# Sums of output weights: made in the prompt attention, or as a GpSimd task in the first half of the projection

## The chip, the cores and the metric

The kernel runs on one core of one Trainium2 chip. The metric is device time in microseconds (us) from the first to the last instruction of the program, with what lies around it; smaller is better. Three runs of the kernel before took 2386.06, 2387.06 and 2393.02 us, median 2387.06.

Engines are called by their names in the profile: PE is TensorE (matmuls, PEld its weight loads), DVE VectorE, ACT ScalarE, POOL GpSimd, SP SyncE, which here only issues DMA transfers.

## What is computed

One layer of a decoder with four head groups, for a prompt of 2048 tokens and for 8 samples of 4 tokens with 8192 cached tokens each. The reference, cut to what matters here:

```python
h = rms_norm(x, pre_g)
z = h @ w_in                                   # (2048 + 32) x 1024 @ 1024 x 5632
ca, cb, cg, pu, pg, q, k, v, sg, mq, mg = split(z)
y_c, conv_new = conv_branch(ca, cb, ...)       # causal depthwise convolution
y_p, pool_new = pool_branch(pu, ...)           # pooling windows 2, 4, 8, 16
y_s = sb_fn(q, k, v, sb_bias)                  # stick-breaking attention, 8 heads x 64
y_m = mem_attend(mq, mk, mv)                   # 4 heads x 128 into 256 memory tokens
mix = concat([y_c * silu(cg), y_p * silu(pg), y_s * silu(sg), y_m * silu(mg)])
out = rms_norm(mix @ w_out, post_g)            # 2048 x 1024 output weights
return x + out
```

The samples attend to cached keys and values, which are gathered page by page through a page table. The last product, `mix @ w_out`, is made with seven products of half-size blocks in place of eight (Strassen's scheme in Winograd's form), so that some products need sums and differences of blocks of `w_out`. These are the sums of output weights that the change moves.

## The kernel before

**Stages.** The program runs through four stages, one behind the other on TensorE.

1. The projection (`z_groups`, called from `main`), up to about 1480 us. It goes over two halves of the prompt tokens, called parts 0 and 1, and in each over groups of 128 output columns: q, k and v first, then per chunk c of 0 to 3 the kinds ca, cb, pu, cg, pg, mg, and mq with sg. For each group `load_w` loads the weights (`wr`, on SyncE's queue), `split_w` splits them into a high and a low part (`whi` on ACT, `wlo` on POOL or, for some, DVE), and `mm3` makes three products per block of 128 rows (L242). Beside it run small generators, the tasks. `Tasks.step` advances each of them once per half group; among them are `mem_attend`, the pooling branch, the convolution and `later_stats`.
2. The attention of the samples (`sample_stages`) is woven into the projection. One of its 64 steps n takes about 18 us: two gathers of cached keys (`kt`, L924), their transposes on DVE (`T`, L957), score matmuls (`sSA`, L970), weights, four gathers of cached values (`vt`, L924) and the values matmuls (`sO`, L1009). The gathers are indirect DMAs that POOL issues in its own order. There is one set of four `vt` buffers, so that the gathers for step n are issued after the values matmuls of step n - 1.
3. The prompt attention (`sb_prompt`), from about 1490 to 1975 us: four head pairs, each with four blocks of 512 query rows. A block's score matmuls are L1253, the gates `gam` and `be` on ACT L1257 and L1258, the scans `E` on DVE L1323 and L1326, the products `be` on POOL L1335, the transposes AT on PE L1346, their evictions `at` L1350 and L1352, the values matmuls `av` L1362. `sbo` (L1367) ends a block.
4. The output product, to the end.

**Side work.** Beside the prompt attention a generator `side_work` is advanced by a fixed amount of attention cost (`PACE`). It holds, in this order: the end of the sample attention, `weight_sums`, the output weights of the first product (`out_weights(1, ...)`: a load `wor`, a cast `wohi` on ACT at L1611 and a difference `wolo` on POOL at L1616, eight times), the first mixed rows, and the convolution's normalisation.

**`weight_sums`.** For each of eight j it loads two blocks of 128 rows of `w_out` (`ws`, two tiles of 4 KB per partition, L1569), makes four sums of 128 x 512 elements on POOL (L1575), and stores the two tiles into a DRAM tensor `wsd` (L1578). `wsd` is read from about 1976 us on, in the output product.

**What sets the order.** TensorE's instructions run in the order in which the program is written. On the other engines and on the DMA queues a scheduler sets the order when the program is built; at run time each engine takes its instructions strictly in that order, and so does each DMA queue. An instruction that waits holds all behind it on its engine.

**Shared buffers.** `k4` hands out tiles of 4 KB per partition from a set of four (`K4 = 4`). `later_stats`, the q and k evictions, and `mem_attend` (`mh`, `pT`, `pL`) use them. `state["att"]` counts the calls of `mem_attend` that have not ended.

Of the kernel before, what the change touches and what calls it, by code (L numbers as in the profile page):

```python
# [8 lines left out]
F32 = mybir.dt.float32  # L9
# [4 lines left out]
ALU = mybir.AluOpType  # L14
# [4 lines left out]
P = 128  # L19
# [68 lines left out]
def kernel(  # L88
# [161 lines left out]
    tasks = Tasks()  # L250
# [7 lines left out]
    def k4(name, shape, dt):  # L258
        return st.tile(shape, dt, tag="k4", name=name, bufs=K4)
# [179 lines left out]
    def half_rows(j):  # L439

        k = 4 + j if j < 4 else j - 4
        return slice(P * (8 + j), P * (9 + j)), slice(P * k, P * k + P)

    def params_and_histories(mp):
        prow = mp.tile([P, 512], F32, tag="ht", name="prow")
# [340 lines left out]
    def z_groups(part, groups, between=None):  # L786

        for g in groups:
            last = part == 0 and g is GROUPS[0][-1]
            fill_w()  # L790
            if last:
                X["free"] = 0
                tasks.add(x_stream(1, XA, lambda n: k4(n, [P, D], F32)))
            opened = [z_open(part, kind, c) for kind, c in g]
            cols = COLS[part]
            for ti, (c0, c1) in enumerate(cols):
                for j, (kind, c) in enumerate(g):
                    while X["done", part] < c1:
                        yield 0.0
                    ps = z_tile(f"z{part}{kind}{c}_{ti}")  # L800
                    half = 2.56 * (c1 - c0) / 512
                    for _ in mm3(ps, *wsplit[(part, kind, c)], xhi, xlo, c0, c1):
                        yield half
                    z_evac(part, kind, c, ti, c0, c1, ps, opened[j])
                    if ti == len(cols) - 1:
                        z_close(part, kind, c, opened[j])
                        del wsplit[(part, kind, c)]
                        fill_w()
                    if last and j == 1:
# [749 lines left out]
    FACTORS = {1: 11, 2: 21, 3: 22}  # L1559
    SUMS = {4: (0, 0), 7: (0, 1), 6: (1, 0), 5: (1, 1)}  # L1560

    def weight_sums(wsp):

        ts = {}
        for j in range(9):
            if j < 8:
                ts[j] = [wsp.tile([P, 2, 512], F32, tag="ws", name=f"ws{j}_{n}", bufs=6) for n in range(2)]
                for t, r in zip(ts[j], half_rows(j)[::-1]):
                    sp.dma_start(t.rearrange("p b n -> p (b n)"), w_out0[r])  # L1569
            yield  # L1570
            if j:
                t, u = ts.pop(j - 1)
                for o, a, b, op_ in ((t[:, 1], t[:, 1], u[:, 1], ALU.subtract), (u[:, 1], u[:, 1], u[:, 0], ALU.subtract),
                                     (u[:, 0], t[:, 1], u[:, 0], ALU.add), (t[:, 0], t[:, 0], u[:, 0], ALU.subtract)):
                    pool.tensor_tensor(out=o, in0=a, in1=b, op=op_)  # L1575
                    yield
                for n, o in enumerate((t, u)):
                    sp.dma_start(wsd[n, j - 1], o)  # L1578
                yield

    def weight_load(prod, j, raw):

        if (prod, j) in seconds:
# [333 lines left out]
    def side_work():  # L1917
        nonlocal opm, conv
        with tc.tile_pool(name="sm", bufs=1, side="left", reuse_waits="tile") as sm2:
            yield from sample_end(sm2, side_ps, S)  # L1920
        with tc.tile_pool(name="wsp", bufs=1, side="left", reuse_waits="tile") as wsp:
            yield from weight_sums(wsp)
        opm = ox.enter_context(tc.tile_pool(name="opm", bufs=1, side="left", reuse_waits="tile"))
        yield from out_weights(1, opm, pool)
        while (3, 0) not in flags:
            yield
        for x in lead_:
            out_load(x)
# [12 lines left out]
        while "centered" not in flags:  # L1941
            next(conv)
            yield
# [195 lines left out]
```

## Time and profile before

| what | value |
|---|---|
| profiled execution | 2387.03 us |
| its span, first to last instruction | 2385.3 us |
| mean granted clock of TensorE | 0.987 |
| TensorE busy | 2283.3 us, 96% |
| VectorE busy | 1717.9 us, 72% |
| GpSimd busy | 1282.7 us, 54% |
| ScalarE busy | 1120.3 us, 47% |
| DMA, mean over the span | 234 GB/s |
| sums of output weights on GpSimd | 32, first at 1563.0, last at 1672.2 us |

How to read it: times inside a run count from the first instruction of the span. The profiled execution has 1.7 us around its span. Busy times of engines overlap. Rows of a timeline give start, duration, engine, line, operation, what is written from what, and in square brackets how long the engine sat idle before it and what ended that. Rows of a table of stretches give, for each engine, the busy time and in parentheses the instructions, then the granted clock of TensorE, the busy share of the DMA engines and their rate.

### The profile page before, as it was taken

What the parts mean: (1) busy time and instruction counts of PE and PEld (TensorE: products, weight loads), DVE (VectorE), ACT (ScalarE), POOL (GpSimd) and SP (SyncE); (2) the same over time, 40 slices, a digit from 0 to 9 for tenths busy, and PEclk for the clock granted to TensorE, in tenths of its full rate; (3) what the DMA queues carried; (4) which work ended last, traced back from release to release, by engine and by line L of the source; (5) the groups of instructions that cost most, each with busy time, mean ns of one, the idle gap of its engine ahead of it and who ended that gap; (6) DMA issues with size and microseconds to landing.
All of it is one profiled execution on the core that took longest, in us unless ns stands there. A gap on an engine that the chain in (4) does not pass through costs nothing. (4 is left out here: it accounts for less than half of the span.)

```text
span 2385.3 us, 42238 instructions
## 1 busy us (share of the span) xinstructions
PE 2283.3 (96%) x16024; PEld 1774.9 (74%) x16024; DVE 1717.9 (72%) x2428; ACT 1120.3 (47%) x1947; POOL 1282.7 (54%) x1322
## 2 busy tenths in 40 slices
PE   7999999999999999999999999799999999989996
PEld 7898888888888677777777777455555557878875
DVE  5342796969657564577787868878888966777897
ACT  5322243242442222234242424788899875444554
POOL 3454545555565555545546462699877763531231
PEclk9999999999999999999999999899999999999999
DMA  6678977878778899987877875667443206866774
GB/s 212 196 257 290 349 270 259 286 249 291 246 262 316 296 327 331 327 283 260 305 263 262 269 268 150 165 201 215 123 107 79 78 19 218 289 196 207 238 236 162
DMA packets 336869, 557.94 MB, mean 234 GB/s; under 512 B 27986, under 2 KB 212434, under 8 KB 320267
## 3 DMA queue, kind: packets, MB, share of 16 engines
q1 hardware_dynamic: 281290, 286.53, 38.7%
q0 software_dynamic: 55376, 268.72, 31.8%
q8 instruction: 126, 2.06, 0.3%
q14 instruction: 77, 0.62, 0.1%
HBM read 465.09 MB, written 90.68 MB: 233 GB/s over the span
## 5 line engine op out<-in xcount | busy, mean ns | idle before, releaser
L957 DVE STREAM_TRANSPOSE T<-kt 128x1024 f32<-128x1024 f32 x256 | 308.7, 1226 | 190.0 <-PE sSA L970 179.0
L924 POOL DMA_INDIRECT vt<-in_cache_v_dram,idv x256 | 252.8, 987 | 261.6 <-PE sO L1009 200.6
L610 DVE SCALAR_TENSOR_TENSOR cacc<-U,par,cacc 128x512 f32<-128x512 f32 x480 | 359.9, 750 | 11.0
L1335 POOL TENSOR_TENSOR be<-be,E 128x512 f32<-128x512 f32 (+3 forms) x316 | 300.7, 963 | 70.0 <-DVE E L1326 22.5
L1326 DVE TENSOR_TENSOR_SCAN E<-gam,cr,ZM 128x513 f32<-128x513 f32 x192 | 233.3, 1264 | 23.3 <-ACT gam L1257 13.9
L924 POOL DMA_INDIRECT kt<-in_cache_k_dram,idk x128 | 128.5, 1004 | 195.0 <-DVE T L957 152.1
L1346 PEld LDWEIGHTS AT<-ident,be 128*128 128x128 f32 x1082 | 118.1, 143 | 137.0 <-ACT at L1352 40.9
L1959 PE MATMUL acc<-wohi,mh 128*128 128x512 f32 (+1 forms) x480 | 193.3, 403 | 1.5 <-ACT mh L1704 0.8
L1257 ACT ACTIVATE gam<-S,nbias_bc 128x1024 f32<-128x1024 f32 (+1 forms) x158 | 170.2, 1077 | 47.3 <-ACT be L1258 15.4
L1959 PE MATMUL acc<-wolo,mh 128*128 128x512 f32 (+1 forms) x480 | 189.0, 394 | 0.0
L1346 PE MATMUL AT<-ident,be 128*128 128x128 f32 x1082 | 161.4, 286 | 20.9 <-DVE at L1350 9.1
L1253 PE MATMUL S<-kT,Q 128*128 128x512 f32 (+1 forms) x632 | 176.5, 403 | 4.8 <-ACT be L1258 4.8
L1959 PE MATMUL acc<-wohi,ml 128*128 128x512 f32 x448 | 176.9, 395 | 4.1 <-DVE ml L1715 4.1
L1258 ACT ACTIVATE be<-S,bias_bc 128x1024 f32<-128x1024 f32 (+1 forms) x158 | 169.1, 1070 | 0.0
L1362 PE MATMUL av<-at,V 128*64 128x512 f32 (+3 forms) x640 | 153.1, 558 | 3.9 <-DVE sbo L1367 3.9
L970 PE MATMUL sSA<-T,W 128*32 128x128 f32 x4096 | 140.5, 277 | 2.3 <-DVE T L957 1.4
L970 PEld LDWEIGHTS sSA<-T,W 128*32 128x32 f32 x4096 | 105.6, 110 | 37.4 <-issue 30.8
L1009 PE MATMUL sO<-vt,saT 128*32 128x512 f32 x1024 | 122.3, 592 | 0.0
L1253 PEld LDWEIGHTS S<-kT,Q 128*128 128x128 f32 x632 | 106.7, 196 | 18.2 <-ACT be L1258 5.4
L1323 DVE TENSOR_TENSOR_SCAN E<-gam,ZM 128x384 f32<-128x384 f32 (+1 forms) x124 | 94.6, 811 | 33.1 <-ACT gam L1257 25.7
L1352 ACT COPY at<-AT 128x512 f32<-128x512 f32 x192 | 108.9, 650 | 20.1 <-PE AT L1346 19.9
L1715 DVE TENSOR_TENSOR ml<-mr,mh 128x512 fp32r<-128x512 f32 x108 | 87.2, 812 | 30.7 <-ACT mh L1704 30.6
(577 smaller groups left out, 6039.9 us busy)
## 6 DMA issues: line engine op xcount, KB each, us to landing
Q<-qd SPq DMA_DIRECT2D x64, 256.0 KB
mr<-mixd SPq DMA_DIRECT2D x32, 512.0 KB
mr<-mixd SPq DMA_DIRECT2D x48, 256.0 KB
xtp<-in_x_prompt_dram SPq DMA_DIRECT2D x16, 512.0 KB
kT<-kd SPq DMA_DIRECT2D x64, 128.0 KB
ws<-in_w_out_dram SPq DMA_DIRECT2D x16, 512.0 KB
wsd<-ws SPq DMA_DIRECT2D x16, 512.0 KB
msd<-mr SPq DMA_DIRECT2D x32, 256.0 KB
```

Of the source, the lines that this page charges most:

```text
L610: dve.scalar_tensor_tensor(out=ps, in0=U[:, a + k : a + k + H], scalar=wd[:, k : k + 1], in1=ps, op0=ALU.mult, op1=ALU.add)
L924: pool.indirect_dma_start(out=dst, out_offset=None, in_=rows, in_offset=bass.IndirectOffsetOnAxis(ap=idx, axis=0))
L957: S["turn"] = dve.transpose(T[:, 2 * hh : 2 * hh + 2].rearrange("p s j t -> p (s j t)"), kt[:, 2 * hh : 2 * hh + 2].rearrange("p s j d -> ...
L970: pe.matmul(sSs[n][32 * g : 32 * g + 32, P * ml : P * (ml + 1)], lhsT=W[:, jj, :], rhs=T[:, :, jj, :], start=i == 0, stop=i == 3, tile_pos ...
L1253: pe.matmul(S[:, j, :w], lhsT=Q[:, x, P * (q2 + j) : P * (q2 + j + 1)], rhs=kt[:, :w], start=x == 0, stop=x == 1)
L1257: act.activation(out=ga, in_=S[:, :, :w], func=AF.Sigmoid, bias=nbias_bc[:, h : h + 1], scale=-1.0)
L1258: act.activation(out=be, in_=S[:, :, :w], func=AF.Sigmoid, bias=bias_bc[:, h : h + 1])
L1326: dve.tensor_tensor_scan(out=E[:, j][:, ::-1], data0=g_[:, j][:, ::-1], data1=ZM[:, 0:1].to_broadcast([P, 513]), initial=carry[hh, q2][:, ...
L1335: pool.tensor_tensor(out=be[:, j, :m], in0=be[:, j, :m], in1=E[:, j, 513 - w : 513 - w + m], op=ALU.mult)
L1346: pe.transpose(ap_[:, P * qt : P * (qt + 1)], A[hp, qb, kc, hh, qt][:, P * r : P * (r + 1)], ident)
L1362: pe.matmul(av[64 * hh : 64 * hh + 64, c], lhsT=V[:, 4 * kc + r, 64 * hh : 64 * hh + 64], rhs=ats.pop((hp, qb, kc, r, hh))[:, c], start=dg ...
L1959: pe.matmul(o[:rows], lhsT=m[a][:, k, :rows], rhs=W[prod, 4 * h + k][w], start=not cont and h == k == n == 0, stop=h == 1 and k == 3 and n ...
```

## The change

`weight_sums` becomes a task of the projection. It takes its tiles from the four shared 4 KB buffers in place of a pool of its own, starts a pair only when no `mem_attend` is open, waits three steps after the loads, and makes the same four sums and two stores per pair. `main` adds the task after the group mg of chunk 0 in part 0; `side_work` no longer calls it, and goes from the end of the sample attention straight to `out_weights(1, ...)`.

```diff
+    def weight_sums():
+
+        for j in range(8):
+            while state["att"]:
+                yield
+            t, u = [k4(f"ws{j}_{n}", [P, 2, 512], F32) for n in range(2)]
+            for o, r in zip((t, u), half_rows(j)[::-1]):
+                sp.dma_start(o.rearrange("p b n -> p (b n)"), w_out0[r])
+            for _ in range(3):
+                yield
+            for o, a, b, op in ((t[:, 1], t[:, 1], u[:, 1], ALU.subtract), (u[:, 1], u[:, 1], u[:, 0], ALU.subtract),
+                                (u[:, 0], t[:, 1], u[:, 0], ALU.add), (t[:, 0], t[:, 0], u[:, 0], ALU.subtract)):
+                pool.tensor_tensor(out=o, in0=a, in1=b, op=op)
+                yield
+            for n, o in enumerate((t, u)):
+                sp.dma_start(wsd[n, j], o)
...
-    def weight_sums(wsp):
-
-        ts = {}
-        for j in range(9):
-            if j < 8:
-                ts[j] = [wsp.tile([P, 2, 512], F32, tag="ws", name=f"ws{j}_{n}", bufs=6) for n in range(2)]
-                for t, r in zip(ts[j], half_rows(j)[::-1]):
-                    sp.dma_start(t.rearrange("p b n -> p (b n)"), w_out0[r])
-            yield
-            if j:
-                t, u = ts.pop(j - 1)
...
     def main():
         yield from z_groups(0, GROUPS[0][4:12])
         tasks.add(later_stats())
-        yield from z_groups(0, GROUPS[0][12:])
+        yield from z_groups(0, GROUPS[0][12:17])
+        tasks.add(weight_sums())
+        yield from z_groups(0, GROUPS[0][17:])
...
             yield from sample_end(sm2, side_ps, S)
-        with tc.tile_pool(name="wsp", bufs=1, side="left", reuse_waits="tile") as wsp:
-            yield from weight_sums(wsp)
         opm = ox.enter_context(tc.tile_pool(name="opm", bufs=1, side="left", reuse_waits="tile"))
```

The new function adds 17 lines near the start, so that lines behind it have numbers higher by 17 in the changed kernel, and behind the place of the old one numbers lower by 2.

TensorE's instructions stand in the same order before and after. The first place is GpSimd's queue in the projection, chunk 1 of part 0, around the values gathers of step 11 of the sample attention (`vt11`), before:

```order
L924 DMA kt12_0_4006<-in_cache_k_dram,idk_1378 128x2048
L924 DMA kt12_1_4093<-in_cache_k_dram,idk_1378 128x2048
L233 TENSOR_TENSOR wlo0pu1_4122<-wr0pu1_3865,whi0pu1_4123 128x1024
L727 TENSOR_TENSOR U0_1_3950<-U0_1_3950,sg0cb1_0_4157 128x384
L924 DMA vt11_0_4184<-in_cache_v_dram,idv_1379 128x1024
```

and after:

```order
L456 TENSOR_TENSOR ws1_0_4118<-ws1_0_4118,ws1_1_4119 128x512
L941 DMA kt12_1_4103<-in_cache_k_dram,idk_1378 128x2048
L233 TENSOR_TENSOR wlo0pu1_4136<-wr0pu1_3875,whi0pu1_4137 128x1024
L456 TENSOR_TENSOR ws2_0_4308<-ws2_0_4308,ws2_1_4309 128x512
L456 TENSOR_TENSOR ws2_1_4309<-ws2_1_4309 128x512
L456 TENSOR_TENSOR ws2_1_4309<-ws2_0_4308,ws2_1_4309 128x512
L456 TENSOR_TENSOR ws2_0_4308<-ws2_0_4308,ws2_1_4309 128x512
L744 TENSOR_TENSOR U0_1_3960<-U0_1_3960,sg0cb1_0_4171 128x384
L941 DMA vt11_0_4199<-in_cache_v_dram,idv_1379 128x1024
```

The four sums of ws1 (the last of them is shown) have come ahead of the gather kt12_1, those of ws2 ahead of vt11. In the same way eight sums, of ws3 and ws4, now stand ahead of the next set vt12, four of ws5 ahead of vt13, one of ws0 ahead of vt7, and eight of ws6 and ws7 around kt19_1, ahead of vt18.

The second place is SyncE's queue at the same time; `mixd` stores rows of the memory attention, `mvn` and `wr` are loads of the projection. Before:

```order
L532 DMA mixd_63<-mo0_0_384_4028 128x3x128
L671 DMA mvn0_1_4947<-mvd_68 128x512
L532 DMA mixd_63<-mo0_0_768_4071 128x2x128
L226 DMA wr0pg1_4126<-in_w_in_dram 128x8x128
L226 DMA wr0mg1_4286<-in_w_in_dram 128x8x128
```

and after:

```order
L549 DMA mixd_63<-mo0_0_384_4038 128x3x128
L451 DMA ws1_0_4118<-in_w_out_dram 128x1024
L451 DMA ws1_1_4119<-in_w_out_dram 128x1024
L451 DMA ws2_0_4308<-in_w_out_dram 128x1024
L549 DMA mixd_63<-mo0_0_768_4081 128x2x128
L451 DMA ws2_1_4309<-in_w_out_dram 128x1024
L459 DMA wsd_70<-ws1_0_4118 128x1024
L459 DMA wsd_70<-ws1_1_4119 128x1024
L688 DMA mvn0_1_5002<-mvd_68 128x512
L451 DMA ws3_0_4494<-in_w_out_dram 128x1024
L226 DMA wr0pg1_4140<-in_w_in_dram 128x8x128
```

Loads of ws1 to ws3 and stores of ws1 have come between the store of the memory attention and the weight load wr0pg1, which now stands behind two stores that wait for GpSimd.

The third place is GpSimd's queue in the prompt attention, head pair 0, the first products of its fourth block. Before:

```order
L1575 TENSOR_TENSOR ws0_0_15534<-ws0_0_15534,ws0_1_15535 128x512
L1335 TENSOR_TENSOR be0_3_3_0_0_15608<-be0_3_3_0_0_15608,E0_3_3_0_0_15670 128x127
L1575 TENSOR_TENSOR ws0_1_15535<-ws0_1_15535 128x512
L1331 COPY cr0_3_3_0_0_15673<-E0_3_3_0_0_15670 128x2
L1335 TENSOR_TENSOR be0_3_3_0_0_15608<-be0_3_3_0_0_15608,E0_3_3_0_0_15670 128x255
L1575 TENSOR_TENSOR ws0_1_15535<-ws0_0_15534,ws0_1_15535 128x512
L1575 TENSOR_TENSOR ws0_0_15534<-ws0_0_15534,ws0_1_15535 128x512
L1575 TENSOR_TENSOR ws1_0_15583<-ws1_0_15583,ws1_1_15584 128x512
L1335 TENSOR_TENSOR be0_3_3_0_2_15637<-be0_3_3_0_2_15637,E0_3_3_0_2_15701 128x383
```

and after:

```order
L1352 TENSOR_TENSOR be0_3_3_0_0_15684<-be0_3_3_0_0_15684,E0_3_3_0_0_15751 128x127
L1348 COPY cr0_3_3_0_0_15754<-E0_3_3_0_0_15751 128x2
L1352 TENSOR_TENSOR be0_3_3_0_0_15684<-be0_3_3_0_0_15684,E0_3_3_0_0_15751 128x255
L1352 TENSOR_TENSOR be0_3_3_0_2_15713<-be0_3_3_0_2_15713,E0_3_3_0_2_15782 128x383
L1348 COPY cr0_3_3_0_2_15785<-E0_3_3_0_2_15782 128x2
L1352 TENSOR_TENSOR be0_3_3_0_2_15713<-be0_3_3_0_2_15713,E0_3_3_0_2_15782 128x511
L1614 TENSOR_TENSOR wolo1_0_15738<-wor1_0_15614,wohi1_0_15737 128x512
L1352 TENSOR_TENSOR be0_3_3_1_0_15748<-be0_3_3_1_0_15748,E0_3_3_1_0_15813 128x127
```

The sums are gone from between the products; a `wolo` of the first output product has come in, the first of eight that stood in head pairs 1 and 2 before.

More of the change, by code (lines that the diff above doesn't have):

```diff
@@ L1560 @@
     SUMS = {4: (0, 0), 7: (0, 1), 6: (1, 0), 5: (1, 1)}
-    def weight_sums(wsp):
-        ts = {}
-        for j in range(9):
-            if j < 8:
-                ts[j] = [wsp.tile([P, 2, 512], F32, tag="ws", name=f"ws{j}_{n}", bufs=6) for n in range(2)]
-                for t, r in zip(ts[j], half_rows(j)[::-1]):
-                    sp.dma_start(t.rearrange("p b n -> p (b n)"), w_out0[r])
-            yield
-            if j:
-                t, u = ts.pop(j - 1)
[L1573 to L1579, printed above, removed]
     def weight_load(prod, j, raw):
```

## The prediction

> **What bounds the kernel now.** I read the page's first part, then a table of stretches, then the waits of TensorE, then the timelines around the two places that the change touches.
>
> ```profile
> PE 2283.3 (96%) x16024; PEld 1774.9 (74%) x16024; DVE 1717.9 (72%) x2428; ACT 1120.3 (47%) x1947; POOL 1282.7 (54%) x1322
> ```
>
> TensorE is busy for 2283.3 of 2385.3 us, and the change gives it no work and takes none away. So the time moves only by what TensorE waits, and GpSimd matters where it makes TensorE wait. The next rows are stretches of the span: two of the projection, three of the prompt attention in which the sums of output weights run now, and two of the same attention without them.
>
> ```profile
> core 0: us, PE busy (x) PEld busy (x) DVE busy (x) ACT busy (x) POOL busy (x), PEclk, DMA share, GB/s
> 400.00:500.00 100.00, 100.00 (x900) 89.25 (x899) 92.30 (x134) 37.33 (x71) 57.72 (x55) 1.00 0.79 268
> 790.00:800.00 10.00, 7.52 (x63) 5.24 (x65) 6.73 (x10) 2.49 (x6) 0.16 (x1) 0.83 0.56 194
> 1563.00:1583.40 20.40, 19.55 (x108) 11.35 (x106) 13.43 (x14) 18.06 (x24) 20.08 (x25) 1.00 0.73 226
> 1583.40:1633.20 49.80, 45.10 (x236) 25.91 (x235) 35.90 (x42) 40.59 (x55) 46.88 (x56) 0.93 0.65 202
> 1666.70:1705.00 38.30, 34.35 (x181) 19.66 (x181) 29.18 (x35) 31.10 (x41) 31.25 (x40) 0.96 0.43 118
> 1781.60:1814.40 32.80, 32.32 (x182) 18.79 (x181) 28.80 (x35) 31.18 (x42) 25.48 (x34) 1.00 0.32 78
> 1814.40:1857.00 42.60, 42.01 (x238) 24.16 (x237) 35.24 (x42) 40.28 (x56) 32.49 (x43) 1.00 0.31 77
> ```
>
> Two things are to be seen. In the projection (400 to 500) TensorE is busy all the time at full clock, so every microsecond that it is made to wait there is added to the time. In the attention equal work takes unequal time: the third block of query rows of a head pair has 181 or 182 matmul records in 1666.7 to 1705.0 and in 1781.6 to 1814.4, the fourth 236 and 238 in 1583.4 to 1633.2 and in 1814.4 to 1857.0. The slow ones are those in which GpSimd is full (46.88 of 49.80) and in which the clock falls below 1.00. The waits of TensorE name GpSimd, first for 1555 to 1680, then for 1680 to 1800:
>
> ```profile
> PE AT L1346 <- POOL be L1335: 6.9, 8, 1.2
> ```
>
> ```profile
> PE AT L1346 <- POOL be L1335: 0.3, 1, 0.3
> ```
>
> The transposes AT wait for the products `be`, and those stand behind the sums in GpSimd's queue.
>
> **The change part by part.** *Removed from the attention.* These are the sums, then the products `wolo` that follow them:
>
> ```profile
> L1575 POOL TENSOR_TENSOR ws<-ws,ws x24: 1270/1286/1302, 1563.0 to 1672.2; 128x512 f32<-128x512 f32 x24
> ...
> L1575 POOL TENSOR_TENSOR ws<-ws x8: 1275/1286/1311, 1564.6 to 1669.4; 128x512 f32<-128x512 f32 x8
> ```
>
> ```profile
> L1616 POOL TENSOR_TENSOR wolo<-wor,wohi x7: 1281/1284/1299, 1706.3 to 1782.9; 128x512 fp32r<-128x512 f32 x7
> ```
>
> 32 sums of 1.286 us are 41.2 us of GpSimd. What they cost TensorE is the difference of equal blocks: 49.8 - 42.6 = 7.2 us, 38.3 - 32.8 = 5.5 us, and for the part of the earlier block after the first sum its idle time, 20.40 - 19.55 = 0.9 us. Together 13.6 us, lost clock included. In the place of the sums comes the next step of the side work, eight casts on ScalarE and eight `wolo` on GpSimd, seven of which stand from 1706 on now, where they cost nothing that the blocks show (1781.6 to 1857.0 hold the last of them). Earlier they come more densely. Bounds: nothing, as there, or the price of a sum, 13.6 / 32 = 0.43 us each, 3.4 us. I take 1.5, between the two. Gain: 13.6 - 1.5 = 12.1 us.
>
> *Added to the projection.* GpSimd's queue also holds the gathers of cache rows there (`kt`, `vt`). A `vt` gather waits until the values matmuls `sO` of the step before have freed its four buffers, and the next `sO` needs it. So what stands ahead of a gather in the queue decides whether TensorE waits. The heaviest place has twenty sums (ws1 to ws5) among these rows of GpSimd:
>
> ```profile
> 381.78 0.94 POOL L924 DMA_INDIRECT kt<-in_cache_k_dram,idk  x1 [3.99 <-DVE T L957]
> 383.54 2.40 POOL L233 TENSOR_TENSOR wlo0pu<-wr0pu,whi0pu 128x1024 fp32r<-128x1024 f32 x1 [0.82 <-ACT whi0pu L232]
> 387.58 0.87 POOL L727 TENSOR_TENSOR U<-U,sg0cb 128x384 f32<-128x384 f32 x1 [1.64 <-ACT sg0cb L725]
> 389.90 0.98 POOL L924 DMA_INDIRECT vt<-in_cache_v_dram,idv  x1 [1.46 <-PE sO L1009]
> ...
> 393.69 0.94 POOL L924 DMA_INDIRECT vt<-in_cache_v_dram,idv  x1 [0.30 <-issue]
> ...
> 399.84 0.98 POOL L924 DMA_INDIRECT kt<-in_cache_k_dram,idk  x1 [3.07 <-DVE T L957]
> ...
> 408.23 1.01 POOL L924 DMA_INDIRECT vt<-in_cache_v_dram,idv  x1 [4.03 <-PE sO L1009]
> ...
> 426.32 0.94 POOL L924 DMA_INDIRECT vt<-in_cache_v_dram,idv  x1 [2.55 <-PE sO L1009]
> ```
>
> The values matmuls that use the gathers of 408.23 and of 426.32, and one that I need later, then the transfer rate microsecond by microsecond from 400 to 440:
>
> ```profile
> 424.16 1.90 PE L1009 MATMUL sO<-vt,saT 128*32 128x512 f32 x16
> ...
> 442.41 1.90 PE L1009 MATMUL sO<-vt,saT 128*32 128x512 f32 x16
> ...
> 542.70 1.90 PE L1009 MATMUL sO<-vt,saT 128*32 128x512 f32 x16
> ```
>
> ```profile
> GB/s 401 221 172 360 270 211 330 118 37 33 242 315 205 295 315 311 340 438 422 229 16 16 16 223 338 81 332 390 304 365 347 336 418 406 410 434 420 390 299 262
> ```
>
> Four gathers start 3.8 us apart from first to last (389.90 to 393.69). The set of 408.23 and the `kt` gather behind it, issued 1.25 us after the last, at about 413.3, have landed when the rate falls to 16 at 420: a flight of 6.8 us. So the slack between landing and use is 424.16 - 412.0 - 6.8 = 5.4 us for the set of 408.23, and 442.41 - 430.1 - 6.8 = 5.5 for that of 426.32. Now the queue's delay against before, with GpSimd's idle time in brackets taken off. Eight sums of 1.29 stand ahead of 389.90; their first loads are issued behind this row of SyncE
>
> ```profile
> 373.73 0.37 SPq L532 DMA_DIRECT2D mixd<-mo  x1
> ```
>
> at about 374.5, and land by the same flight at 381.3, so that the idle 3.99 ahead of 381.78 buys only 0.5. Delay 10.3 - 0.5 - 0.82 - 1.64 - 1.46 = 5.9. Eight more stand ahead of 408.23: 5.9 - 3.07 + 10.3 - 4.03 = 9.1; TensorE is late by 9.1 - 5.4 = 3.7. Four more (5.1) ahead of 426.32: 9.1 - 2.55 + 5.1 = 11.7; TensorE is late by 11.7 - 5.5 = 6.2 in all. This is the larger of the two, not their sum, since a late TensorE gives the queue time to catch up. The next set has no sums ahead of it, and the delay ends there. SyncE's queue holds the weight loads of the projection behind the stores of the sums, thus behind GpSimd. I add nothing for them, since a whole group of matmuls lies between such a load and its use; if that cover is gone, the split of the weights on GpSimd comes late by the same delay, and TensorE by no more than it.
>
> Clock: the row of 790 has one wait, 10.00 - 7.52 = 2.5 us, and a mean clock of 0.83 over 10 us, so a wait of this size can cost another 1.7 us. Of my two waits (3.7, then 2.5 more) both could; what the first costs comes off the second, so at most one 1.7 is left. The Trainium skill, in TensorE: Matmul & The Clock Gate, Part 1, says that the clock halves only after an idle window of some 3.4 us; by that rule the row of 790 would stand at 1.00, and the trace differs. By the rule the term is 0, by the row up to 1.7 us.
>
> Traffic: the page gives the transfers of the sums.
>
> ```profile
> ws<-in_w_out_dram SPq DMA_DIRECT2D x16, 512.0 KB
> wsd<-ws SPq DMA_DIRECT2D x16, 512.0 KB
> ```
>
> They fall beside the gathers now. The price on a gather lies between nothing and the bytes that overlap it at the highest rate of the row above: stores of ws3 and ws4 and loads of ws5 are six of 0.52 MB, 3.1 MB at 438 GB/s, 7.2 us. I take 1.8 for traffic and clock together, near the low end, since the same row has pauses of 16 to 37 to fill. Sum for this place: 6.2 + 1.8 = 8.0 us.
>
> The first pair (ws0) stands ahead of a gather that idles longer:
>
> ```profile
> 305.38 0.94 POOL L924 DMA_INDIRECT vt<-in_cache_v_dram,idv  x1 [5.00 <-PE sO L1009]
> ```
>
> One sum and the wait for its load hold it back by some 5 us (the load is issued some 3 us before this row, and flies 6.8), about the slack of the other sets, 5.4: 0, and as much as the load comes later if it does. The last pairs (ws6, ws7) stand around these:
>
> ```profile
> 524.89 0.87 POOL L727 TENSOR_TENSOR U<-U,sg0cb 128x384 f32<-128x384 f32 x1 [2.81 <-ACT sg0cb L725]
> 527.26 0.98 POOL L924 DMA_INDIRECT vt<-in_cache_v_dram,idv  x1 [1.51 <-PE sO L1009]
> 530.36 0.95 POOL L924 DMA_INDIRECT vt<-in_cache_v_dram,idv  x1 [2.12 <-PE z0cb L242]
> ```
>
> 10.3 - 2.81 - 1.51 - 2.12 = 3.9 us of delay against a slack of 542.70 - 532.9 - 6.8 = 3.0 (two more gathers, 1.25 apart, follow 530.36): TensorE waits 0.9, call it 1.0; with two overlapping stores of each pair, 2.1 MB at 438 GB/s, up to 5.8.
>
> **Sum.** The profiled execution took 2387.03 us (span 2385.3 and 1.7 around it), and the median of the runs is 2387.06, so both are the same base. 2387.0 - 12.1 + 8.0 + 1.0 = 2383.9: 2384 us.
>
> **The rivals.** *The gathers stay hidden (faster).* If a gather alone flies faster than 6.8 us (2.1 MB at 438 GB/s is 4.8), the slack of the last set is 7.5 and TensorE is late by 11.7 - 7.5 = 4.2; with no traffic term, nothing at the last pairs, and `wolo` as cheap as it is now, 2387.0 - 13.6 + 4.2 = 2377.6. For it: the pauses in the rate. Against it: the flight was read with the queue as full as it is.
>
> *The transfers collide (slower).* Loads and stores of the sums share the DMA engines with the gathers where the rate is already near 438. Then the heavy place costs 6.2 + 7.2 + 1.7 = 15.1 and the last pairs 5.8 + 1.7 = 7.5, and 2387.0 - 12.1 + 22.6 = 2397.5. It decides from 19.3 us of loss on (12.1 + 7.2). The Trainium skill, in DMA: Bandwidth & Descriptors, Queues, rings and completion order, says that each engine takes turns between queues, packet by packet. By that rule a gather loses at most as many bytes of time as the other queue has moved meanwhile, which is this rival's price.
>
> *The room in the attention is filled again.* If the dense `wolo` and casts hold `be` as the sums did, the gain is 5 and the time 2387.0 - 5 + 9.0 = 2391. For it: ScalarE is busy 40.28 of 42.60 in the undisturbed block. Against it: that block lost nothing.
>
> **How the numbers follow.** A measurement of this kernel tells 0.3%, 7.2 us, from no change. Forecast (gain and loss nearly cancel) 0.44, hidden gathers 0.28, collision 0.20, filled room 0.08. The likeliest ends at 2384, its own range 2379.8 (no change's lower edge) to 2394.2. The hidden case is faster; the collision is slower; of the filled room half is slower and half no change; of the forecast 0.02 is taken as slower. That gives faster 0.28, same 0.46, slower 0.26. The range takes in both outer cases with some room for the bounds: 2374 to 2400.
>
> **What would show it.** Right: the blocks that took 49.8 and 38.3 take about 42.6 and 32.8; TensorE reaches the projection's step of 442.41 later by 5 to 14 us, with idle time ahead of `sO` around 424 and 442, and the step of 542.70 later by little more. Wrong: `sO` keeps its times (the hidden case), the delay goes on growing after 450 (collision, or a weight load behind a store), or the attention blocks keep waiting for `be`.

## The result, and the profile after

The changed kernel takes 2396.7 us (median of 7 runs, 2393.8 to 2408.5), the kernel before 2388.2 in the same runs: a ratio of 1.0042, 95% interval 1.0029 to 1.0054. The forecast was 2384.0 and "no change that can be measured"; the kernel is slower, inside the range, near the rival in which the transfers collide (2397.5). The profiled execution spans 2394.2 us against 2385.3.

The first row of the changed kernel's page, each engine's busy time:

```profile
PE 2286.9 (96%) x16024; PEld 1769.5 (74%) x16024; DVE 1719.3 (72%) x2428; ACT 1116.5 (47%) x1947; POOL 1278.5 (53%) x1322
```

The matmuls are the same 16024 in the same order, so the two traces can be laid beside each other matmul by matmul. I call the start of a matmul in one kernel's trace less its start in the trace of before TensorE's *lag*:

| at (us of before) | 285 | 350 | 440 | 620 | 1480 | 1970 | 2340 |
|---|---|---|---|---|---|---|---|
| changed kernel | -0.5 | -1.1 | 15.6 | 22.1 | 18.5 | 3.4 | 8.9 |
| no sums at all (first experiment) | 1.8 | 2.0 | 2.9 | 2.8 | 1.2 | -13.6 | -9.6 |

The attention gives 15.1 us back (18.5 to 3.4). The projection takes 22 at the two places forecast. Of these 4 return between 780 and 860, but 3.1 return there without sums too: it is the kernel before that stops there, at the row of 790. The 5.5 us behind 1970 need not be the change's: the kernel without sums loses 4.0 there, the other kernels below between 0 and 9, and `sums_first`, whose sums stay in the attention, 3.1. The finish seems to scatter, and to have been quick in the profiled execution of before; the first experiment leaves this open.

The stretches of the changed kernel: the heavy place of the projection, then the blocks that took 49.8 and 38.3 us:

```profile
core 0: us, PE busy (x) PEld busy (x) DVE busy (x) ACT busy (x) POOL busy (x), PEclk, DMA share, GB/s
...
404.00:424.00 20.00, 16.02 (x88) 8.09 (x88) 11.78 (x16) 1.65 (x4) 17.55 (x16) 0.74 0.90 345
...
1598.90:1643.10 44.20, 42.39 (x238) 24.14 (x237) 35.51 (x43) 42.70 (x61) 36.92 (x48) 1.00 0.39 108
1676.40:1709.20 32.80, 32.32 (x182) 18.83 (x181) 28.84 (x35) 30.39 (x40) 24.22 (x33) 1.00 0.31 78
```

The blocks now take 44.2 and 32.8 us at full clock. In 404 to 424 TensorE waits 4.0 us, and its clock is 0.74, which costs up to another 5.2 (20 x 0.26). What it waits for from 380 to 620, and what SyncE's queue waits for at the stores of the sums from 290 to 560 (us in total, times, longest):

```profile
PE sO L1026 <- DMA vt<-in_cache_v_dram,idv: 4.5, 5, 2.6
PE sSA L987 <- DVE T L974: 2.7, 1, 2.7
```

```profile
SPq L459 <- POOL ws L456: 45.2, 10, 12.0
```

GpSimd's queue ahead of the gathers that were issued from 389.90 to 393.69 before:

```profile
375.94 0.94 POOL L941 DMA_INDIRECT kt<-in_cache_k_dram,idk  x1 [0.30 <-issue]
384.87 1.29 POOL L456 TENSOR_TENSOR ws<-ws,ws 128x512 f32<-128x512 f32 x1 [8.00 <-DMA ws<-in_w_out_dram]
...
390.38 0.95 POOL L941 DMA_INDIRECT kt<-in_cache_k_dram,idk  x1
...
400.14 0.97 POOL L941 DMA_INDIRECT vt<-in_cache_v_dram,idv  x1
...
403.90 0.94 POOL L941 DMA_INDIRECT vt<-in_cache_v_dram,idv  x1 [0.30 <-issue]
```

GpSimd stands 8.00 us at the first sum of ws1, whose load has not landed, with the gather `kt` behind it. The `vt` gathers go out 10.2 us later than before, and TensorE then takes them one by one:

```profile
407.70 1.42 PE L1026 MATMUL sO<-vt,saT 128*32 128x512 f32 x2 [2.64 <-DMA vt<-in_cache_v_dram,idv]
409.78 1.92 PE L1026 MATMUL sO<-vt,saT 128*32 128x512 f32 x2 [0.66 <-DMA vt<-in_cache_v_dram,idv]
412.34 5.59 PE L1026 MATMUL sO<-vt,saT 128*32 128x512 f32 x12 [0.64 <-DMA vt<-in_cache_v_dram,idv]
```

The load of ws1 went out at 373.85, so that 11.0 us passed from its issue to the first sum. The last `vt` gather went out at 403.90, 8.4 us before the last matmuls that waited. At this set the lag goes from -1.2 to 10.3, and by 440 to 15.6, as the next set comes late too. The weight load `wr0mg` goes out at 411.3 here, 7.2 us later than before, and no cast waits for it: what reaches TensorE at this place is late gathers.

### The profile page after: what moved, and what is told of

Read it like the earlier page. It is cut to its first block, busy times and chain, and to the rows that moved or that the text cites. A ratio compares the mean times of both kernels' runs of the same rounds, so it can differ in the third digit from the quotient of the medians.

```text
span 2394.2 us, 42247 instructions
## 1 busy us (share of the span) xinstructions
PE 2286.9 (96%) x16024; PEld 1769.5 (74%) x16024; DVE 1719.3 (72%) x2428; ACT 1116.5 (47%) x1947; POOL 1278.5 (53%) x1322
## 5 line engine op out<-in xcount | busy, mean ns | idle before, releaser
L627 DVE SCALAR_TENSOR_TENSOR cacc<-U,par,cacc 128x512 f32<-128x512 f32 x480 | 360.0, 750 | 11.1
L1026 PE MATMUL sO<-vt,saT 128*32 128x512 f32 x1024 | 134.6, 603 | 4.5 <-DMA vt<-in_cache_v_dram,idv 4.5
```

The lines of the kernel that those rows point to most:

```text
L627: dve.scalar_tensor_tensor(out=ps, in0=U[:, a + k : a + k + H], scalar=wd[:, k : k + 1], in1=ps, op0=ALU.mult, op1=ALU.add)
```

## The experiments

Each was timed beside the kernel before on the same chip; ratios are to that, with 95% intervals, and "us" is a difference of ratios times 2388. An interval of 0.0013 on either side makes such a difference good to some 4 us.

### What the sums, the bytes and the waits cost, each by itself

My first theory: GpSimd stands at sums whose loads have not landed, and the gathers queue behind it. Rivals: the execution of the sums, and the bytes.

```diff
 no_sums
-        tasks.add(weight_sums())
```


> The sums are made nowhere: the task is left out, and the finish reads unsummed weights of the same size in their place, so its products are not the reference's. Every theory expects the whole gain of the attention and none of the loss: 2388.2 - 15.1 (what TensorE's lag fell by in the attention) = 2373 if the 5.5 us that the changed kernel lost in the finish are scatter between executions, and 2378 to 2379 if they belong to the change. TensorE reaches the attention at the time of the kernel before, within 2 us.

0.9955 (0.9942 to 0.9969), 10.7 us faster than before. By the runs that is the whole gain, and the changed kernel's loss is 1.0042 - 0.9955, 20.8 us. The trace gives 14.8 in the attention and takes 4.0 back in the finish. By the ratio the time is 2377.5 (0.9955 x 2388.2), nearer to the 2378 to 2379 at which the finish's loss belongs to the change than to the 2373 of scatter; with the loss of `sums_first` against it, that stays open.

```diff
 sums_only: no load, no store
-                pool.tensor_tensor(out=o, in0=a, in1=b, op=op)
+                pool.tensor_tensor(out=o, in0=x, in1=x, op=op)     # x: 512 columns of xhi
```


> GpSimd executes the 32 sums at the same places of the program, on an operand that is already in memory, with no load and no store (the finish reads unsummed weights, so the output is not the reference's). Theory (standing at loads): 41 us of execution remain but no standing, so the loss is the forecast's queue terms or less, 3 to 8 us, time 2376 to 2381. Rival (the execution itself holds the gathers back): 15 us or more of loss, 2388 or more. Rival (transfers): no loss, 2373 to 2375.

0.9984 (0.9971 to 0.9997): 6.9 us over no sums, about what the forecast's queue terms had (6.2 + 1.0). But a sum took 1.03 us here, not 1.29, and TensorE does not wait for `sO`, as the forecast had it. From 380 to 440 the lag grows by 4.0, at one wait of 2.7 us with half clock behind it, for the transposes of keys. That the numbers agree is luck.

```profile
PE sSA L983 <- DVE T L970: 2.7, 1, 2.7
```

```diff
 transfers_only: loads and stores as they are
-                pool.tensor_tensor(out=o, in0=a, in1=b, op=op)
                 yield
```


> The task loads and stores as in the changed kernel, but GpSimd adds nothing (the stored weights are the raw ones, so the output is not the reference's). Theory (GpSimd stands at a sum whose own load has not landed, and the gathers queue behind it): without a sum there is nothing to stand at, the loss in the projection falls from 19 us to 2 to 5, time 2375 to 2379. Rival (the transfers delay the gathers): most of the 19 us stays, 2388 or more.

1.0025 (1.0012 to 1.0038): 16.7 us with no sum to stand at. My theory falls as the whole cause. Where the time goes is told by four answers: SyncE's waits at the stores (290 to 460), its loads of the weights `wr0mg` before and here, who waits for them, and TensorE's waits:

```profile
SPq L457 <- DMA ws<-in_w_out_dram: 41.0, 9, 9.0
```

```profile
L226 SPq DMA_DIRECT2D wr0mg<-in_w_in_dram x1: 372/372/372, 404.1 to 404.1; - x1
```

```profile
L226 SPq DMA_DIRECT2D wr0mg<-in_w_in_dram x1: 379/379/379, 437.9 to 437.9; - x1
...
  ACT whi0mg L232: 19.3, 1
```

```profile
PE z0pg L242 <- DVE sg0cg L724: 11.7, 1, 11.7
PE z0mg L242 <- DVE sg0pg L716: 6.7, 1, 6.7
```

SyncE stands at nine of the stores until the load has landed, with the weight loads behind it: `wr0mg` goes out at 437.9 and not at 404.1. ScalarE comes to the cast of these weights and stands 19.3 us, and behind the cast in its queue lie the activations that empty TensorE's PSUM banks. So TensorE waits 11.7 us for a bank before it needs the late weights, and the lag grows by 14.0 from 424 to 440. The wait of 6.7 us stands near 320, where kernels without a sum in this half wait up to 1.9 as well. To see whether bytes or held queues do this, I took the store's wait away at the same bytes, then the bytes at the same waits:

```diff
 bytes_no_wait: the sixteen stores of transfers_only
-                sp.dma_start(wsd[n, j], o)
+                sp.dma_start(wsd[n, j], xhi[:, 0:2, :512].bitcast(F32))
```


> The transfers alone with the same bytes at the same places of SyncE's queue, but each store takes its data from a tile that is long in memory, so that SyncE waits neither for a load nor for a sum (no sums are made, and the output is not the reference's). Theory A (held queues): 6 to 11 us below the kernel before, as without sums. Theory B (bytes): as the transfers alone were, 2 to 5 us above the kernel before, since the bytes come as densely or more so.

0.9993 (0.9981 to 1.0006): 9.1 us over no sums, 7.6 less than with the wait at the store; the wait of 11.7 us is gone. But the edit moved more than the wait. Stores that wait for nothing had been set far ahead in SyncE's queue when the program was built. First transfers_only, then here:

```profile
L457 SPq DMA_DIRECT2D wsd<-ws x16: 319/326/4073, 302.8 to 554.5; - x16
```

```profile
L457 SPq DMA_DIRECT2D wsd<-xhi x16: 519/690/1236, 79.4 to 152.5; - x16
```

Half the bytes have left the tight place with the wait. The lag is 8.1 us at 285, before the first load of the sums (300.6), and grows by 4.2 from there to 620. So the 9.1 is not the price of the bytes where the changed kernel has them, and the 7.6 not that of the wait alone.

```diff
 small_transfers: sums as in sums_only; 16 columns loaded and stored
-                sp.dma_start(o.rearrange("p b n -> p (b n)"), w_out0[r])
+                sp.dma_start(o[:, :, :16], w_out0[r].rearrange("p (b n) -> p b n", b=2)[:, :, :16])
...
-                sp.dma_start(wsd[n, j], o)
+                sp.dma_start(wsd[n, j, :, :, :16], o[:, :, :16])
```


> Every queue entry and wait of the changed kernel, with few bytes: SyncE loads 16 columns of each half of a tile, GpSimd makes the four sums of full width on an operand in memory, SyncE stores 16 columns of what they made (the finish reads unsummed weights, so the output is not the reference's). Theory A (the two queues hold each other: GpSimd stands at a sum for SyncE's load, SyncE at a store for GpSimd's sum): nearly the loss of the changed kernel, 3 to 8 us above the kernel before. Theory B (it takes the bytes: flights of loads and gathers get longer, and only then the queue's delay passes the slack): as the sums alone, 2 to 5 us below the kernel before.

1.0003 (0.9990 to 1.0017): 11.5 us, between the two expectations; with hardly a byte the waits between the queues add 4.6 us to the sums, by a difference good to about as much. GpSimd stands for these loads too, in all and at ws1:

```profile
POOL ws L456 <- DMA ws<-in_w_out_dram: 19.7, 3, 8.0
```

```profile
385.41 1.04 POOL L456 TENSOR_TENSOR ws<-xhi 128x512 f32<-128x512 f32 x1 [7.99 <-DMA ws<-in_w_out_dram]
```

The second load of ws1 went out by 375 here, with one part in 32 of the bytes, and the sum again waited over 10 us from then. So at this place GpSimd waits neither for SyncE to issue the load nor for the load's many bytes; what makes so small a load so slow is not shown. From 380 to 440 the lag grows by 0.0 us with no sums, 4.0 with sums alone, 12.0 here and 16.6 in the changed kernel. That is one execution of each, but by it most of the loss at this place comes with the sums and the waits, without the bytes.

```diff
 apart: bytes_no_wait, and 32 sums from xhi into a tile of their own
+                pool.tensor_tensor(out=v, in0=x, in1=x, op=op)
```


> Sums and bytes together, but without a wait between them: GpSimd makes the 32 sums on an operand that is long in memory, SyncE loads and stores the same bytes at the same places, and neither waits for the other (the output is not the reference's). Against no sums, the sums alone cost 0.0029 of the time (7 us) and the bytes alone 0.0038 (9 us). If the parts add up and the holding of the queues is the rest, the ratio to the kernel before is 0.9955 + 0.0067 = 1.002, against 1.0042 of the changed kernel. If the holding costs nothing once both are there, 1.004. If sums and bytes hide behind the same waits, 0.999 to 1.000.

1.0009 (0.9998 to 1.0020): sums and bytes together cost 12.9 us, and the changed kernel 7.9 more. Here too the stores ran far ahead (76.9 to 154.7), and a sum took 1.04 us and not 1.29. In all:

| | no wait between the queues | with the waits | difference |
|---|---|---|---|
| sums, few bytes | 6.9 | 11.5 | 4.6 |
| bytes, no sums (stores moved on the left) | 9.1 | 16.7 | 7.6 |
| both (stores moved on the left) | 12.9 | 20.8 | 7.9 |

Only the first row is free of moved stores, and its difference is at the edge of what these runs can tell. What they show of the changed kernel is that the sums' transfers, with all that waits for them, cost 13.9 us (20.8 - 6.9), the longer sums included; how much of it is bytes and how much waits stays open.

### Mending the waits where the task stands

```diff
 longer_lead, between a pair's loads and its first sum
-            for _ in range(3):
+            for _ in range(10):
                 yield
```


> The changed kernel with ten steps in place of three between the load of a pair and its first sum; all else as there, and the output is the reference's. Theory (standing at loads): the waits of 8.0 and 5.6 us of GpSimd for the loads go, and the loss falls from 19 us to under 10, time 2380 to 2387. Rivals (execution, transfers): the same sums and bytes, so 2392 to 2397. If the buffers that a pair now holds for longer are missed by other work, TensorE waits elsewhere, and the time says so.

1.0043 (1.0027 to 1.0059), a miss: the lag at 440 is 6.0 in place of 15.6, but 16.1 at 620 and 17.2 at 1480. GpSimd still stands 7.2 us ahead of the first sum of ws1. The `vt` gathers go out 0.9 us earlier (399.27), TensorE waits 1.6 us for them and not 4.0, and its clock stays at 1.00, so that this set costs 5 us and not 11.5. The later pairs, now later still, met the next tight places.

```diff
 transfers_late: transfers_only; late_stores: the changed kernel; both ahead of the stores
+            for _ in range(6):
+                yield
             for n, o in enumerate((t, u)):
                 sp.dma_start(wsd[n, j], o)
```


> The transfers alone again (no sums, so the output is not the reference's), the same bytes, but six steps between a load and its store, so that SyncE finds the load landed when it comes to the store. Theory (SyncE's queue is held at the store, and the weight loads and the stores of results behind it come late): the 16 us of the run with transfers alone shrink to 2 to 6, time 2381 to 2385. Rival (the bytes themselves delay gathers and weights): 2391 to 2396 as before.

> The changed kernel with six more steps between the sums of a pair and its store; loads and sums as there, the output is the reference's. Theory (SyncE held at stores): SyncE no longer waits for GpSimd's sums, loads go out earlier, and of some 18 us of loss (2396.7 against 2379.0 with no sums) the 7 of the sums alone and little more stay: 2384 to 2389. Rival (bytes): 2394 to 2398. Rival (GpSimd standing for loads that fly long): 2390 to 2395.

The transfers: 0.9983 (0.9970 to 0.9997), as expected in number, but not by the whole of the reason given. SyncE stood at the stores longer than before, from 290 to 560, first here and then in transfers_only:

```profile
SPq L459 <- DMA ws<-in_w_out_dram: 60.3, 11, 10.7
```

```profile
SPq L457 <- DMA ws<-in_w_out_dram: 54.1, 12, 9.0
```

The total that SyncE stands is thus no measure of the loss; what it holds back, and when, is. Here `wr0mg` went out at 422.1, where transfers_only had 437.9:

```profile
L226 SPq DMA_DIRECT2D wr0mg<-in_w_in_dram x1: 384/384/384, 422.1 to 422.1; - x1
```

No cast waited for it, and the lag stays at 8.8 from 400 to 440, where it grew by 14.0 in transfers_only. At this late weight load the two runs part; by the ratios they are 10.0 us apart. How much of its lateness is the waits at the stores, and how much the pairs that come closer together there, is not told apart.

The changed kernel: 1.0048 (1.0034 to 1.0061), a miss. SyncE still waits for the sums at the stores, 39.5 us:

```profile
SPq L461 <- POOL ws L456: 39.5, 8, 11.9
```

```diff
 gpsimd_stores
-                sp.dma_start(wsd[n, j], o)
+                pool.dma_start(wsd[n, j], o)
```


> The changed kernel with the sixteen stores issued from GpSimd's queue behind the sums that make them, not from SyncE's; loads, sums and bytes as there, the output is the reference's. Theory (SyncE held): the same gain as with late stores less some 16 us of GpSimd time for issuing in gaps of its queue, 2385 to 2392. Rival (bytes): 2394 or more, since nothing else changes.

1.0064 (1.0042 to 1.0086), a miss. No store is in SyncE's queue now, and SyncE stands for the buffers instead, which come free when GpSimd's stores have landed:

```profile
SPq L451 <- DMA wsd<-ws: 35.1, 5, 17.9
```

```diff
 spread_sums: the task is no longer among the tasks; in sample_stages, with two sums a step
             turn(n + 1, 0)
+            if n >= 6:
+                next(ws, None)
             yield
```


> Loads, sums and stores of a pair are tied to the steps of the sample attention: the load in one step, two sums behind the gathers of the next, two behind those of the one after, the stores a step later, from the seventh step on; the output is the reference's. So GpSimd never stands for a load, SyncE never for a sum, and no sum stands directly ahead of the gathers of values. Theory (queues held): nearly the whole gain, 2379 to 2384, faster than both kernels. Rival (bytes): the same bytes over three times the time, 2385 to 2392. Two of the four shared buffers are held nearly all the time; if that is missed, TensorE waits for the memory attention or the convolution.

1.0053 (1.0033 to 1.0072), 17 us or more above what the theory gave. From 290 to 760 SyncE stands 35.7 us at the stores, and GpSimd 11.1 us at one sum:

```profile
SPq L461 <- POOL ws L456: 35.7, 8, 11.8
```

```profile
POOL ws L456 <- ACT sbe L1002: 11.1, 1, 11.1
```

None of the four that keep the sums is faster than the changed kernel, and in the trace of each TensorE, SyncE or GpSimd still stands for a pair.

### Other places for the sums

```diff
 second_half (queries_half: GROUPS[1][8])
-        tasks.add(weight_sums())
...
+        yield from z_groups(1, GROUPS[1][7:18])
+        tasks.add(weight_sums())
+        yield from z_groups(1, GROUPS[1][18:-2])
```


> The changed kernel with the task started at the second half's first repetition of the convolution groups but one (about 1120 us in place of 290 us), the output is the reference's. There a set of gathers lands 6 to 9 us before its use in the trace of the changed kernel, against 5 to 6 us at 380 to 440 us, and the DMA engines move 270 GB/s against 350. If slack and room for bytes decide, the loss in the projection falls to 3 to 10 us and the time is 2 to 8 us below the kernel before; if every place is as tight, it is as the changed kernel, 6 to 10 us above.

> The changed kernel with the task started with the queries of the second half (about 940 us), where no convolution runs on VectorE yet, but the DMA engines move 340 GB/s; the output is the reference's. Theory B (bytes) expects more loss here than in the run that starts at 1120 us, theory A (held queues) the same or less, since SyncE has fewer stores to hold there.

1.0003 (0.9986 to 1.0020) and 1.0087 (1.0057 to 1.0117). The place decides: the same task costs 11.5 us over no sums from 1137 on, and 31.5 from 939 on. The theory of the bytes expected this: in the kernel before the DMA engines move 297 GB/s from 921 to 1210 and 275 from 1113 to 1430. But the longest waits of the dear place (11.6 and 4.3 us) are in the samples' memory attention, which stands there, so that bytes are not shown as the cause. In the cheaper one TensorE waits for `T`, which `kt` gathers feed:

```profile
PE sSA L987 <- DVE T L974: 10.4, 5, 3.9
```

```diff
 second_half_loose (loose_earlier: 4 and 4)
+        yield from z_groups(1, GROUPS[1][7:11])
+        tasks.add(weight_sums())
...
-            for _ in range(3):
+            for _ in range(6):
                 yield
...
                 sp.dma_start(wsd[n, j], o)
+            for _ in range(6):
+                yield
```


> The task in the second half (from about 1000 us), with six steps in place of three between loads and sums and six steps between pairs, so that one pair at most stands ahead of a set of gathers; the output is the reference's. The run that started at 1120 us lost 16 us of lag, 9 of them where sums of one pair stood beside another's transfers at 1195 to 1216 and 4.5 at 1295, and nothing at three other pairs. If it is density that costs, the loss is 5 to 9 us and the ratio to the kernel before 0.996 to 0.999; if each pair costs the same wherever it is, 1.000.

1.0035 (1.0022 to 1.0048), outside what either theory gave. In its trace the lag grows by 6.1 us from 939 to 1480, past seven pairs (989 to 1395); then the eighth, drained behind the last group, has GpSimd standing 28.31 us for its loads, the second of which goes out at 1494, and the first scores of the attention wait 11.11:

```profile
1501.29 1.26 POOL L456 TENSOR_TENSOR ws<-ws,ws 128x512 f32<-128x512 f32 x1 [28.31 <-DMA ws<-in_w_out_dram]
```

```profile
1512.63 1.65 PE L1272 MATMUL S<-kT,Q 128*128 128x512 f32 x3 [11.11 <-ACT be L1277]
```

```diff
 seven_one: the loose run; other_sums makes the eighth pair in the attention, as the kernel before makes all
-        for j in range(8):
+        for j in range(7):
...
+            yield from other_sums(wsp)
```


> As the loose run in the second half, but its last pair, which came at 1501 us, behind the last group of the projection, is made in the prompt attention instead; the output is the reference's. In the loose run's trace TensorE's lag was 4.4 us at 1480 us, and the first scores of the attention then waited 11.1 us. If that wait was the last pair's, the ratio to the kernel before falls from 1.0035 to 0.996 to 0.999; if the seven pairs cost what they did in the first half, 1.001 to 1.004.

> The loose run in the second half with four steps in place of six before the sums and between pairs, so that the eighth pair comes some four steps of the sample attention before the end of the projection and not behind it; the output is the reference's. Same reading: 0.996 to 1.000 if it was the last pair's place, 1.001 to 1.004 if not.

With that one pair in the attention 0.9978 (0.9967 to 0.9988), faster than both kernels: a single pair at the wrong place had cost 0.0057, 13.6 us more than in the attention. With four steps in place of six loose_earlier was 1.0001 (0.9989 to 1.0012): better than the loose run by 8 us, but the closer pairs cost more in the projection (from 939 to 1480 the lag grows by 11.3).

```diff
 shared_out: pairs 0, 1, 3, 6 in the second half, the others in the attention
+    EARLY = (0, 1, 3, 6)
...
+            if j not in EARLY:
+                for _ in range(7):
+                    yield
+                continue
...
+            yield from other_sums(wsp)
 sums_first: the kernel before
+            yield from weight_sums(wsp)
             yield from sample_end(sm2, side_ps, S)
-            yield from weight_sums(wsp)
```


> Four of the eight pairs stay in the prompt attention, with twice the room between their sums, and four are made in the second half of the projection, at the places where the run that started at 1120 us lost nothing; the output is the reference's. If the loss grows faster than the number of sums on both sides, a half costs less than half: 2 to 4 us of the attention's 13 and 0 to 4 in the projection, ratio to the kernel before 0.996 to 0.998. If each pair has its price wherever it is, half of either: 1.000.

> The kernel before, with the sums ahead of the end of the sample attention in the side work, not behind it: they start some 60 us earlier in the prompt attention, where GpSimd is busy 66 of 100 us, and the output is the reference's. If what counts is GpSimd's room where the sums stand, they cost less there, 2 to 8 us below the kernel before. If TensorE waits for `be` wherever 32 sums come at one in 3.4 us, the time is that of the kernel before.

0.9955 (0.9943 to 0.9966), 10.7 us faster than the kernel before and the best of all. In its trace the lag is 2.6 us at 1480 (1.2 with no sums), so the four pairs of the projection cost next to nothing. The sixteen sums in the attention ran from 1565 to 1609, no further apart in time than before, and 8.0 of 14.8 us were gained there: half the sums, about half the price, in one execution, the slowest of the six. By the runs it is no slower than no sums at all (0.9955 both), so that the price of the half that stays is not settled. It wins by free places in the projection, not by more room between the sums in the attention. Sums ahead of the sample's end: 1.0007 (0.9997 to 1.0018), so an earlier place in the attention is worth nothing that can be measured.

## Why the prediction was wrong

**The gain** was read from the right rows. The blocks forecast at 42.6 and 32.8 take 44.2 and 32.8, and the wait of AT for `be` no longer stands in the list. For 12.1 the lag gives 15.1, the runs 10.7. The first block's 1.6 us over the forecast are about the 1.5 allowed for denser `wolo`; that `wolo` costs them is not shown.

**"By the same flight"** is the step that failed first. The sum had the load of ws1 land at 381.3, after 6.8 us, hence a delay of 5.9 at the first set of gathers, about the slack of the next sets (5.4 and 5.5), and no lateness there. On the chip the first sum started at 384.87, 11.0 us behind its load's issue, the delay was 10.2, the gathers took 8.4, and TensorE stood from 405.1 to 407.70, a set earlier than the prediction had it. This set alone cost 11.5 us, the place to 440 16.8, where the sum had 8.0 for all of it. The queue terms (6.2 and 1.0) are near the 6.9 of the sums alone by luck: in that run TensorE waits elsewhere.

**Traffic and clock** were put at 1.8 us together, "near the low end", and **"I add nothing for them"** at 0 for the weight loads behind SyncE's stores. What stands in place of these 1.8 is 13.9 us: the changed kernel costs that much more than its sums alone. At the heavy place the clock alone is up to 5.2 of it, where I allowed 1.7 and took less. The split between bytes and waits stays open, since the runs without waits moved the stores. Of the weight loads, transfers_only shows that the cover named, a group of matmuls between a load and its use, is no cover: the cast of the weights stands on ScalarE ahead of the activations that free PSUM, and one late load cost 14.0 us. In the changed kernel's own trace no cast waits for the two weight loads of this place, so the zero was unsafe, but not what failed here.

**The last pairs** (1.0, up to 5.8) cost about 6: the lag goes from 15.6 at 440 to 22.1 at 620, 5.0 of it from 520 to 566. The first stop there is 2.7 us for `T`, behind `kt` gathers that the sum left out. ws0 cost nothing, as forecast.

**The chances.** The forecast's loss was 9.0, the rival's 22.6, and the changed kernel lost 20.8 by the runs. The rival in which the transfers collide had 0.20. Its number is near; its price was made of bytes and clock alone, and in small_transfers, with hardly a byte, 12.0 of the 16.6 us from 380 to 440 are lost as well. The sign named for it, a delay that goes on growing after 450, is weak: 0.8 us from 440 to 520, then the 5.0 of the last pairs.

## What to carry to other kernels

When a step moves, list for each in-order queue what it will now stand at, and what stands behind that: a load that feeds a sum and a store that waits for it tie two queues together, and transfers and ties cost twice as much here as the sums. A late load hurts first where an engine stands for it ahead of other work, not where the data is used. Price a small task by its place: four pairs cost next to nothing in the second half, and one 13.6 us behind its end. When an experiment takes a wait away, look where the built program has put what waited: here the freed stores ran 220 us earlier and more.

## What the runs showed of the hardware that was not expected

The clock fell behind a stop of 2.64 us and stayed at half through waits of 0.66 and 0.64 us, though TensorE worked most of the time. Two microseconds a row, the granted clock is the column behind the busy times:

```profile
406.00:408.00 2.00, 0.30 (x1) 0.20 (x2) 0.96 (x2) 0.00 (x0) 1.83 (x3) 1.00 0.98 387
408.00:410.00 2.00, 1.34 (x3) 0.20 (x2) 1.93 (x3) 0.84 (x2) 1.99 (x4) 0.58 1.03 422
...
416.00:418.00 2.00, 2.00 (x7) 0.32 (x2) 0.00 (x0) 0.00 (x0) 2.00 (x2) 0.50 0.98 386
418.00:420.00 2.00, 2.00 (x10) 2.00 (x11) 1.78 (x2) 0.00 (x0) 2.00 (x3) 0.86 0.89 264
```

The matmuls `sO` of this set, then those of two sets in the kernel before (ns, least, median, most):

```profile
L1026 PE MATMUL sO<-vt,saT x16: 646/1061/1070, 407.7 to 416.9; 128*32 128x512 f32 x16
```

```profile
L1009 PE MATMUL sO<-vt,saT x32: 592/592/592, 387.8 to 407.4; 128*32 128x512 f32 x32
```

A stop for late transfers is thus paid more than twice here: 4.0 us of waiting and up to 5.2 of half speed in these 20 us. In longer_lead the same set came with waits of 0.98, 0.18, 0.22 and 0.17 us, and the clock stayed at 1.00. The Trainium skill, TensorE: Matmul & The Clock Gate, Part 1, has the clock fall after an idle window of some 3.4 us and rise after a busy one. The trace fits the second: TensorE is busy without a stop from 412.34 on, and the clock rises between 418 and 420. It does not fit the first taken as the length of one wait, since none here was that long.
